# Conformer front end of a two-layer trunk: first product in high and low parts, the wide convolution wholly on the matrix engine

## The chip, the cores and the metric

The kernel runs on one NeuronCore of a Trainium2 chip. The engines are TensorE (PE in the profile; PEld is its weight load), VectorE (DVE), ScalarE (ACT) and GpSimd (POOL); SyncE (SP) issues the large transfers. Each engine works through its own instructions in order and waits for the others by semaphores. The metric is the device time of one execution in microseconds (us). Three executions of the kernel before took 2595.46, 2598.17 and 2601.18 us; the median is 2598.17 us.

## The reference

The input is one sequence of 256 positions and 2048 channels in float32. Two layers follow each other; each has a token mixer and a dense squared-ReLU MLP, each with a pre-RMSNorm whose shift, scale and gate come from a conditioning vector c. Only the first mixer, the Conformer convolution module, is touched by the change:

```
def conformer_conv(u, w_pw1, b_pw1, w_dw, b_dw, ln_g, ln_b, w_pw2, b_pw2):
    v = u @ w_pw1 + b_pw1
    a, gt = jnp.split(v, 2, axis=-1)
    v = a * jax.nn.sigmoid(gt)
    v = causal_dwconv(v, w_dw, b_dw)
    v = jax.nn.silu(layernorm(v, ln_g, ln_b))
    return v @ w_pw2 + b_pw2
...
        mod = (sc @ w_mod[i] + b_mod[i])[:, None, :]
        sh1, sc1, g1, sh2, sc2, g2 = jnp.split(mod, 6, axis=-1)
        u = rmsnorm(h, norm_mix_g[i]) * (1 + sc1) + sh1
```

So u is 256 x 2048, w_pw1 is 2048 x 4096, the depthwise convolution has 31 taps over each of 2048 channels, and w_pw2 is 2048 x 2048. The modulation vectors (sh1, sc1, g1, sh2, sc2, g2) are products of silu(c) with a 2048 x 12288 matrix per layer.

## The kernel before

Activations lie with channels on the 128 partitions and the 256 positions along the row, four channel tiles to a group. A channel tile of 128 is called a row here, as in the code; there are 16. Weights come in tiles of 128 x 2048 numbers (1 MB) through SP's queue, in program order, into three buffers `w32`.

**Modulation vectors.** `gemv` (L263 to L293) reads a 1 MB tile of w_mod into one of the buffers `wm` (2) or `hid` (4). Most tiles are multiplied with silu(c) and summed by one DVE instruction (L289). The groups in `PE_GROUPS` go through four PE products with 32 columns (L280), and after every fourth tile a copy, four transposes (L301) and a short DVE sum in `columns`. POOL adds the bias (`mod_done`, L317 to L320). A list of such tiles, `EARLY`, is worked off by `pump` at the rates `RATE_PW1`, `BETWEEN`, `RATE_PW2`, `RATE_OPEN` and so on.

**The first product** (w_pw1) has eight column blocks of 512 (two rows of a, two of the gate) and four quarters of the 2048 inputs. `native` multiplies in plain float32 (L709): 16 products of 128 x 128 by 128 x 256 for each weight tile. The opening takes blocks 0 to 3 together, quarter by quarter, since the shift and scale of a quarter (eight w_mod tiles, all summed on DVE) are loaded between the weights; `vectors` (L576) makes u of a quarter from them. Blocks 4 to 7 follow one by one.

**The gate** (`glu`) is a sigmoid on ACT (L590) and one DVE instruction (L592), which writes the row into a padded buffer `vpad`, kept behind u in the same tile.

**The wide convolution** takes two ways. Eight rows (`TE_ROWS`) go to PE: POOL's queue copies the row into four shifted copies (`shift`, L632; rows 14 and 15 by PE in `lift`, L640) and loads a matrix of taps from memory (L624), and `convolve` (L655) makes 32 products with 32 columns. The other eight rows are done by `conv`: 28 taps on ACT (L602), summed by DVE (L611), three more on DVE. `close` (L669, L672) subtracts a common mean and squares; `moments` and `direct` sum for the LayerNorm.

**The second product** (w_pw2) and the later ones split each weight tile in two halves, each into a high part (`wh`, ACT, L358) and a low part (`wl`, DVE, L360), three buffers each. With x split the same way, `products` in its `single` form makes three PE products of 128 x 256 for one: wh by x high, wh by x low, wl by x high (L373). A half of `wl` can only be written when the products of the half three places earlier have been made.

The order on each engine is made by a scheduler from program order and priorities (`high_priority`, `issue_after`); transfers keep program order.

Of the kernel before, what the change touches and what calls it, by code (L numbers as in the profile page):

```python
# [15 lines left out]
P = 128  # L16
# [13 lines left out]
def spread(n, slots):  # L30
# [16 lines left out]
RATE_PW1 = [1, 1, 1, 1, 1, 2, 1, 1, 1, 2, 1, 1, 1, 1, 0, 0]  # L47
BETWEEN = 5
# [11 lines left out]
ACT_TAPS = 28  # L60


TE_ROWS = (3, 5, 6, 7, 9, 13, 14, 15)
# [3 lines left out]

EARLY = [(0, s, 4 * g + i) for s, g in ((G1, 0), (G1, 1), (G1, 2), (SC2, 0), (SH2, 0), (SH2, 1)) for i in range(4)]
_te = [(0, SH2, 5 + i) for i in range(11)]
_ve = [(0, G1, 12 + i) for i in range(4)] + [(0, SC2, 4 + i) for i in range(12)]  # L70
EARLY = EARLY[:-3] + [v for pair in zip(_ve[:9], _te) for v in pair] + _te[9:] + _ve[9:]


PE_GROUPS = {(0, SH2, g) for g in range(4)}
# [5 lines left out]
    ("b_pw1", 32), ("w_dw", 16 * TAPS), ("b_dw", 16), ("ln_g", 16), ("ln_b", 16), ("b_pw2", 16),  # L80
# [21 lines left out]
def layout(inp):  # L102
# [8 lines left out]
    for ct in TE_ROWS[:-2]:  # L111
        order[ct] = order[ct].reshape(32, 4).T.reshape(-1)
    order = order.reshape(-1)
    par = np.concatenate([
        _cols(a["c"]), _cols(a["b_mod"]), _cols(a["norm_mix_g"]), _cols(a["norm_mlp_g"]),
        _cols(a["final_norm_g"]), _cols(a["cf_b_pw1"]),
        a["cf_w_dw"][0].reshape(TAPS, NT, P).transpose(2, 1, 0).reshape(P, -1),
# [19 lines left out]
    taps = np.zeros((32, D), f)  # L137
    taps[:TAPS] = a["cf_w_dw"][0].reshape(TAPS, D)
    quad = np.zeros((len(TE_ROWS), 4, 32, 8, 4, 32), f)
    for i, ct in enumerate(TE_ROWS):  # L140
        w = taps[:, ct * P:(ct + 1) * P].reshape(4, 8, 32, 4)
        if ct >= NT - 2:
            w = w.reshape(4, 8, 4, 32).transpose(0, 1, 3, 2)
        for p in range(32):
            quad[i, :, p, :, :, p] = w[:, :, p, :]
    return {
        "quad": quad.reshape(len(TE_ROWS), P, 8, P),
# [29 lines left out]
class Trunk:  # L177
# [44 lines left out]
    def prologue(self):  # L222
# [26 lines left out]
        self.xpad = self.const("xpad", [P, 5 * (3 + T)])  # L249
        self.sel = self.t("bT", [P, T], bufs=1)[:, :P]  # L250
# [12 lines left out]
    def gemv(self, layer, seg, ct, parts=((0, 4),)):  # L263
# [8 lines left out]
        if (layer, seg, g) in PE_GROUPS:  # L272
# [10 lines left out]
            if i == 3:  # L283
                row = self.t("t2", [P, 512], bufs=3)
                with self.tc.issue_after(self.act):
                    nc.scalar.copy(out=row, in_=self.row_sums)
                self.rows_left.append([self.row_sums, row, m, layer, seg, g, 0])
# [63 lines left out]
    def split_half(self, w, i, hi_after=None, lo_after=None):  # L351
        nc = self.nc
        s = slice(2 * i, 2 * i + 2)
        wh = self.wp.tile([P, 2, 512], F32R, tag="wh", name=self.nm("wh"), bufs=3)
        wl = self.wp.tile([P, 2, 512], F32R, tag="wl", name=self.nm("wl"), bufs=3)
# [192 lines left out]
    def conformer(self):  # L548
# [12 lines left out]
        room = [self.b("u", [P, 8 * T]) for _ in range(4)]  # L561
        u = [v[:, :4 * T].rearrange("p (k t) -> p k t", k=4) for v in room]

        W = T + TAPS
        vpad = [v[:, 4 * T + i * W:4 * T + (i + 1) * W] for v in room for i in range(3)]
        for v in vpad:
            nc.gpsimd.memset(v[:, :TAPS - 1], 0.0)
            nc.gpsimd.memset(v[:, W - 1:], 0.0)
        dd = [self.b("acc", [P, 4, T], bufs=5) for _ in range(4)]
        st = {"m0": None, "sq": {}, "sums": None}  # L570

        quad = self.b("acc", [P, 8, P], bufs=5)
        copies = self.xpad[:, :4 * LONG].rearrange("p (c t) -> p c t", c=4)
        parts, late = {}, []

        def vectors(g, t0, t1):  # L576

            for t in range(t0, t1):
# [4 lines left out]
                nc.scalar.activation(out=u[g][:, t, :], in_=m, func=AF.Identity,  # L583
                                     bias=self.mod_tile(0, SH1, g)[:, t:t + 1])

        def glu(ct, bank):

            with self.tc.high_priority(AHEAD_GLU if ct < NT - 3 else AHEAD_CHAIN):
# [101 lines left out]
        def native(blocks, done, pump=None, hook=None, rows=()):  # L690
# [24 lines left out]
            if len(blocks) == 1:  # L715
                for g in range(4):
                    if hook and g == 3:
                        hook()
# [657 lines left out]
```

## Time and profile before

| quantity | value |
|---|---|
| median of three executions | 2598.17 us |
| the profiled execution | 2596.74 us |
| its span | 2594.8 us |
| PE busy over the span | 2541.4 us (98%) |
| DVE busy | 1911.0 us (74%) |
| ACT busy | 1308.0 us (50%) |
| mean DMA rate | 256 GB/s |
| first product begins / blocks 0 to 3 end | 37.19 / 152.23 us |
| `lift` of rows 14 and 15 begins | 288.13 us |
| second product begins | 311.24 us |

Times are in us from the start of the span. A view by lines groups instructions by source line, engine and tile; "idle before" names what ended the wait. A plain float32 product appears as two records of PE. The chain of waits follows the work that ended last backwards. The view by windows gives the busy time of each engine in a stretch, the granted PE clock and the share of time the DMA engines were busy.

### The profile page before, as it was taken

The numbers are of one execution on the slowest core, as the hardware profiler recorded it, in microseconds if no ns is written. First come the engines' busy times: TensorE is split into PE (matmuls) and PEld (weight loads), VectorE is DVE, ScalarE is ACT, GpSimd is POOL, SyncE is SP. The second block draws the span as 40 slices with busy tenths as digits, with TensorE's granted clock in tenths as the row PEclk, the third lists the DMA queues.
The fourth block names the chain that finished last, engine by engine and source line by source line (L and its number), as shares of the span: only waits on it lengthen the run. The fifth ranks groups of instructions, "written<-read, shape, count | busy, mean of one in ns | idle before, by whom it ended". The sixth has DMA issues, their size and how long they took to land.

```text
span 2594.8 us, 36897 instructions
## 1 busy us (share of the span) xinstructions
PE 2541.4 (98%) x14671; PEld 2183.1 (84%) x14671; DVE 1911.0 (74%) x2460; ACT 1308.0 (50%) x2009; POOL 147.5 (6%) x212
## 2 busy tenths in 40 slices
PE   6999999999999999999999999999999999999998
PEld 5887698988888888888888888888998888888886
DVE  6579577877878878888777777888885555565565
ACT  2067453544434434447777767644454444443443
POOL 0011000000000000000000000000001101101000
PEclk8999999999999999999999999999999999999999
DMA  9988797788888878856555555678765555555554
GB/s 404 381 321 305 266 345 292 276 325 324 311 327 319 321 291 345 320 215 218 185 188 176 176 185 186 243 297 324 284 252 195 190 184 195 192 182 195 193 182 144
DMA packets 94895, 664.85 MB, mean 256 GB/s; under 512 B 10977, under 2 KB 10977, under 8 KB 16769
## 3 DMA queue, kind: packets, MB, share of 16 engines
q1 hardware_dynamic: 89138, 643.87, 67.5%
q0 software_dynamic: 5152, 16.97, 2.3%
q8 instruction: 115, 1.88, 0.3%
q10 hardware_dynamic: 432, 1.66, 0.2%
q14 instruction: 58, 0.48, 0.1%
HBM read 657.02 MB, written 2.20 MB: 254 GB/s over the span
## 4 chain that ended last, share of the span: by engine, by line
PE 95%; DVE 2%; DMA 2%; ACT 1%; issue 0%; POOL 0%; ACTq 0%; SPq 0%; DVEq 0%
PE mm L373 59%; PE mm L427 8%; PE mm L429 8%; PE mm L428 8%; PE mm L709 7%; DMA hid<-wmT 1%; PE mm L655 1%; PE ms L709 1%; PE ms L1288 1%; PE ms L280 1%; DVE wl L360 0%; DVE hid L289 0%; PE ms L1257 0%; PE ms L1267 0%; PE ms L509 0%
## 5 line engine op out<-in xcount | busy, mean ns | idle before, releaser
L373 PE MATMUL mm<-u,wh 128*128 128x512 f32 (+1 forms) x4544 | 1374.2, 365 | 6.4 <-ACT u L482 2.3
L358 ACT CAST wh<-w 128x1024 fp32r<-128x1024 f32 x768 | 806.7, 1051 | 991.5 <-PE mm L373 612.1
L360 DVE TENSOR_TENSOR wl<-w,wh 128x1024 fp32r<-128x1024 f32 x768 | 941.2, 1228 | 495.6 <-ACT wh L358 492.0
L373 PE MATMUL mm<-u,wl 128*128 128x256 f32 x3840 | 1080.0, 282 | 0.1
L373 PEld LDWEIGHTS mm<-u,wh 128*128 128x128 f32 x4544 | 812.8, 190 | 157.8 <-issue 10.2
L373 PEld LDWEIGHTS mm<-u,wl 128*128 128x128 f32 x3840 | 730.2, 190 | 5.6 <-issue 3.4
L427 PE MATMUL mm<-wh,hid 128*128 128x512 f32 x896 | 350.9, 392 | 0.0
L429 PE MATMUL mm<-wh,hid 128*128 128x512 f32 x896 | 348.9, 389 | 0.0
L428 PE MATMUL mm<-wl,hid 128*128 128x512 f32 x896 | 348.8, 389 | 0.0
L289 DVE SCALAR_TENSOR_TENSOR wm<-wm,scb 128x2048 f32<-128x2048 f32 x133 | 303.7, 2283 | 11.0 <-DMA wm<-wmT 10.7
L709 PE MATMUL mm<-u,w 128*128 128x256 f32 x864 | 192.3, 384 | 19.1 <-ACT u L583 19.1
L709 PEld LDWEIGHTS mm<-u,w 128*128 128x128 f32 x864 | 165.2, 192 | 45.3 <-ACT u L583 19.9
L427 PEld LDWEIGHTS mm<-wh,hid 128*128 128x128 f32 x896 | 168.2, 188 | 35.7 <-issue 1.0
L428 PEld LDWEIGHTS mm<-wl,hid 128*128 128x128 f32 x896 | 168.2, 188 | 35.4 <-issue 0.7
L429 PEld LDWEIGHTS mm<-wh,hid 128*128 128x128 f32 x896 | 168.2, 188 | 35.2
L373 PE MATMUL mm<-hid,wh 128*128 128x512 f32 (+1 forms) x576 | 183.7, 376 | 2.8 <-DVE acc L913 2.8
L373 PE MATMUL mm<-hid,wl 128*128 128x256 f32 x512 | 143.9, 281 | 0.0
L289 DVE SCALAR_TENSOR_TENSOR hid<-hid,scb 128x2048 f32<-128x2048 f32 x43 | 98.2, 2285 | 40.7 <-DMA hid<-wmT 40.6
L373 PEld LDWEIGHTS mm<-hid,wh 128*128 128x128 f32 x576 | 104.9, 190 | 24.0 <-DVE acc L913 3.2
L317 POOL TENSOR_TENSOR mod<-mod,par 128x4 f32<-128x4 f32 x46 | 39.5, 858 | 1139.8 <-DVE wm L289 905.7
L602 ACT ACTIVATE taps<-u,par 128x256 f32<-128x256 f32 x224 | 93.0, 501 | 9.4 <-DVE taps L611 7.0
L373 PEld LDWEIGHTS mm<-hid,wl 128*128 128x128 f32 x512 | 97.4, 190 | 0.4 <-issue 0.2
(251 smaller groups left out, 1599.7 us busy)
## 6 DMA issues: line engine op xcount, KB each, us to landing
w<-w SPq DMA_DIRECT2D x256, 1024.0 KB, 4.9
wm<-wmT SPq DMA_DIRECT2D x139, 1024.0 KB, 7.3
w<-win SPq DMA_DIRECT2D x80, 1024.0 KB, 4.9
hid<-wmT SPq DMA_DIRECT2D x53, 1024.0 KB, 11.1
w<-pw SPq DMA_DIRECT2D x46, 1024.0 KB, 7.5
w<-wout SPq DMA_DIRECT2D x32, 1024.0 KB, 6.7
acc<-ac_d POOLq DMA_DIRECT2D x16, 512.0 KB, 7.5
xpad<-u POOLq DMA_DIRECT2D x24, 131.5 KB, 9.0
```

The source lines that it names most:

```text
L280: self.pe = nc.tensor.matmul(self.row_sums[32 * t:32 * t + 32, :], lhsT=self.scol[:, kt:kt + 1].broadcast_to([P, 32]), rhs=w[:, t * 512:(t ...
L289: self.sum = nc.vector.scalar_tensor_tensor(out=w, in0=w, scalar=1.0, in1=self.scb, op0=ALU.mult, op1=ALU.mult, accum_out=m[:, i:i + 1]).ins
L317: nc.gpsimd.tensor_tensor(out=m, in0=m, in1=b, op=ALU.add)
L358: nc.scalar.copy(out=wh, in_=w[:, s, :])
L360: nc.vector.tensor_tensor(out=wl, in0=w[:, s, :], in1=wh.bitcast(F32), op=ALU.subtract)
L373: self.pe = self.nc.tensor.matmul(out, lhsT=lhsT, rhs=rhs, skip_group_check=True, **kw).ins
L427: mm(banks[q], lhsT=hi, rhs=wh[:, k, :], start=g == 0 and t == 0, stop=False)
L428: mm(banks[q], lhsT=hi, rhs=wl[:, k, :], start=False, stop=False)
L429: mm(banks[q], lhsT=lo, rhs=wh[:, k, :], start=False, stop=g == 3 and t == 3)
L602: st["tap"] = nc.scalar.activation(out=p4[:, q, :], in_=vp[:, k + q:k + q + T], func=AF.Identity, scale=self.col("w_dw", ct * TAPS + k + q ...
L655: self.pe = nc.tensor.matmul(o[32 * c:32 * c + 32, :], lhsT=w[:, k, 32 * c:32 * c + 32], rhs=r[:, c, k:k + T], start=k == 0, stop=k == 7, ...
L709: self.pe = nc.tensor.matmul(o, lhsT=w[:, t, j * P:(j + 1) * P], rhs=u[g][:, t, :], start=g == 0 and t == 0 and j < 2, stop=g == 3 and t == 3,
```

## The change

The first product takes the split form of the later ones: u is written in high and low parts (`split_x`, ACT and DVE), each weight tile of w_pw1 is split in two halves, and each product becomes three. All 16 rows of the convolution go through `convolve`; `conv` on ACT and DVE is gone. The matrix of taps is no longer read from memory: one DVE instruction (`weigh`) multiplies a diagonal pattern with the taps. Rows lie unpadded in the place where the closed row will stand; `shift` copies only what exists, and zeros are written once into the two buffers of copies (one of which, with one matrix of taps, takes the two `wm` buffers during blocks 4 to 7). From the third of these weight tiles on, one row is convolved after each tile. The PE groups of the modulation change: the first two of sh1 and the last two of sh2 in place of all four of sh2. `EARLY` is reordered: 24 tiles, all for DVE, are worked off in blocks 4 to 7 (16 before), 4 in `BETWEEN` (5 before), and in the second product the next 18 hold 3 for PE (9 before).

```diff
-RATE_PW1 = [1, 1, 1, 1, 1, 2, 1, 1, 1, 2, 1, 1, 1, 1, 0, 0]
-BETWEEN = 5
+RATE_PW1 = [1, 2] * 8
+BETWEEN = 4
...
-PE_GROUPS = {(0, SH2, g) for g in range(4)}
+PE_GROUPS = {(0, SH1, 0), (0, SH1, 1), (0, SH2, 2), (0, SH2, 3)}
...
+        self.diag32 = self.xpad[:, 4 * LONG:4 * LONG + 32]
+        nc.vector.reduce_sum(out=self.diag32, in_=self.ident.rearrange("p (a j) -> p j a", a=4),
+                             axis=mybir.AxisListType.X)
...
-                nc.scalar.activation(out=u[g][:, t, :], in_=m, func=AF.Identity,
-                                     bias=self.mod_tile(0, SH1, g)[:, t:t + 1])
+                self.split_x(u[g], t, m, self.mod_tile(0, SH1, g)[:, t:t + 1])
...
-        def conv(ct):
...
+        def weigh(ct):
+            nc.vector.tensor_tensor(
+                out=quads[ct % 2].rearrange("p k (c j) -> p (k c) j", j=32),
+                in0=self.diag32.rearrange("p (o j) -> p o j", o=1).broadcast_to([P, 32, 32]),
+                in1=self.col("w_dw", ct * 32, 32).rearrange("p (k o) -> p k o", o=1).broadcast_to([P, 32, 32]),
+                op=ALU.mult)
         def shift(ct):
-            weigh(ct, quad, nc.gpsimd)
             for i in range(4):
-                nc.gpsimd.dma_start(out=copies[32 * i:32 * i + 32], in_=vpad[ct % 12][:, 8 * i:8 * i + LONG])
+                k = TAPS - 1 - 8 * i
+                n = min(T, LONG - k)
+                nc.gpsimd.dma_start(out=copies[ct % 2][32 * i:32 * i + 32, :, k:k + n],
+                                    in_=dd[ct // 4][:, ct % 4, :n])
...
+        def products(banks, b, g, parts, ts):
+            for j in (0, 2, 1, 3):
+                o = banks[j % 2][:, (j // 2) * T:(j // 2 + 1) * T]
+                for t in ts:
+                    self.products(o, parts[t // 2], u[g], t % 2, t, slice(j * P, (j + 1) * P), True,
+                                  g == 0 and t == 0 and j < 2, g == 3 and t == 3)
+                if g == 3 and ts[-1] == 3 and j >= 2:
+                    glu(2 * b + j - 2, banks[j - 2])
...
+        for b in range(FIRST, 8):
+            if b >= 6:
+                moments(b - 6)
+            own = [self.bank(self.mm, "mm") for _ in range(2)]
+            for g in range(4):
+                w = self.load_w(a["pw1"][b, g])
+                self.pump(pump(g))
+                pair = [ahead(w, k) for k in range(2)]
+                for k in range(2):
+                    products(own, b, g, pair, (2 * k, 2 * k + 1))
+                if b == FIRST and g < 2:
+                    continue
+                ct = next(row)
+                if ct == 1:
+                    common()
+                    close(0)
+                convolve(ct)
+                weigh(ct + 2)
+                if ct + 2 < LIFTED:
+                    shift(ct + 2)
+                if ct:
+                    close(ct)
```

Line numbers of the changed kernel are a few lower: its L286 is L289 before (sum of a w_mod tile), L357 is L360 (low part of a weight half), L566 is L580 (`nrm`, the scaled row), L483 writes the low part of u, L578 is L592 (gate), L594 is L632 (copies). Two places show what moves.

The order on DVE around the third quarter of the opening. `hid` and `wm` are w_mod tiles, `nrm` the scaled rows, `wl` low parts; the first fence is before, the second the change.

```order
L289 SCALAR_TENSOR_TENSOR hid_404,mod_380<-hid_404,scb 128x2048
L289 SCALAR_TENSOR_TENSOR hid_407,mod_384<-hid_407,scb 128x2048
L289 SCALAR_TENSOR_TENSOR wm_428,mod_380<-wm_428,scb 128x2048
L289 SCALAR_TENSOR_TENSOR hid_431,mod_384<-hid_431,scb 128x2048
L289 SCALAR_TENSOR_TENSOR hid_452,mod_380<-hid_452,scb 128x2048
L580 SCALAR_TENSOR_TENSOR nrm_462<-h_77,mod_380,t_16_160 128x256
```

```order
L286 SCALAR_TENSOR_TENSOR wm_728,mod_600<-wm_728,scb 128x2048
L286 SCALAR_TENSOR_TENSOR hid_731,mod_604<-hid_731,scb 128x2048
L357 TENSOR_TENSOR wl_737<-w_98_734,wh_736 128x1024
L357 TENSOR_TENSOR wl_741<-w_98_734,wh_740 128x1024
L286 SCALAR_TENSOR_TENSOR hid_792,mod_600<-hid_792,scb 128x2048
L566 SCALAR_TENSOR_TENSOR nrm_802<-h_77,mod_600,t_16_161 128x256
L566 SCALAR_TENSOR_TENSOR nrm_806<-h_77,mod_600,t_16_161 128x256
L286 SCALAR_TENSOR_TENSOR wm_798,mod_604<-wm_798,scb 128x2048
L483 SCALAR_TENSOR_TENSOR u_165<-nrm_802,mod_604,u_165 128x256
```

Before, DVE met only w_mod tiles and scaled rows there; now two low parts stand between each pair of w_mod tiles, and each row of u ends with a DVE instruction.

The order on DVE of the change where blocks 0 to 3 end and block 4 begins. The `mm` and `ms` tiles are the sums of blocks 0 to 3 in PSUM (two for a block), `hid_1386` is a w_mod tile, and `w_178` is the first weight tile of block 4. Before, the plain product of block 4 needed no DVE instruction of its own.

```order
L578 SCALAR_TENSOR_TENSOR acc_1237<-mm_237,par,a_1320 128x256
L286 SCALAR_TENSOR_TENSOR hid_1386,mod_1388<-hid_1386,scb 128x2048
L578 SCALAR_TENSOR_TENSOR acc_1238<-mm_238,par,a_1329 128x256
L578 SCALAR_TENSOR_TENSOR acc_1238<-mm_239,par,a_1338 128x256
L578 SCALAR_TENSOR_TENSOR acc_1238<-ms_464,par,a_1347 128x256
L578 SCALAR_TENSOR_TENSOR acc_1238<-ms_465,par,a_1356 128x256
L357 TENSOR_TENSOR wl_1391<-w_178_1384,wh_1390 128x1024
```

The gates of all eight rows, the last of which need the end of block 3's products, now stand ahead of the low part that block 4's first products read.

On ACT of the change, in the same place: `a_1347` and `a_1356` are the sigmoids of the last two rows, and `wh` high parts of the first two weight tiles of block 4.

```order
L575 ACTIVATE a_1347<-ms_464,par 128x256
L355 CAST wh_1394<-w_178_1384 128x1024
L355 CAST wh_1454<-w_184_1446 128x1024
L575 ACTIVATE a_1356<-ms_465,par 128x256
L355 CAST wh_1458<-w_184_1446 128x1024
```

Two casts now stand between the last two sigmoids.

More of the change, by code (lines that the diff above doesn't have):

```diff
@@ L560, in conformer @@
         nc.scalar.activation(out=r, in_=ps, func=AF.Sqrt, scale=1.0 / D, bias=self.eps)
[L561 to L569, printed above, removed]
+        u = [self.b("u", [P, 4, 2 * T], F32R) for _ in range(4)]
         st = {"m0": None, "sq": {}, "sums": None}
-        quad = self.b("acc", [P, 8, P], bufs=5)
-        copies = self.xpad[:, :4 * LONG].rearrange("p (c t) -> p c t", c=4)
-        parts, late = {}, []
+        parts = {}
         def vectors(g, t0, t1):
@@ new lines, in ahead, with vec @@
+        def ahead(w, i, room=None):
+            with self.tc.high_priority(self.ahead):
+                return self.split_half(w, i, room=room)
+        def vec(g, t):
+            for s in (SC1, SH1):
+                self.gemv(0, s, 4 * g + t, ((0, 2), (2, 3), (3, 4)) if g == 3 else ((0, 4),))
+        for t in range(4):
+            vec(0, t)
+            if t == 1:
+                with self.tc.issue_after(self.sum):
+                    nc.vector.reciprocal(r, r)
+        self.columns()
@@ new lines, in conformer @@
+        vectors(3, 0, 2)
+        room = lambda tag: self.b("acc", [P, 2, 512], F32R, bufs=5)
+        last = []
+        for i in range(FIRST):
+            if i == 2:
+                vec(3, 2)
+                vectors(3, 2, 3)
+            w = self.load_w(a["pw1"][i, 3])
+            first = ahead(w, 0, room)
+            last.append([first, ahead(w, 1, None if i < 3 else room)])
+            products(banks[i], i, 3, last[i], (0, 1))
+        vec(3, 3)
+        vectors(3, 3, 4)
+        dd = [self.b("acc", [P, 4, T], bufs=5) for _ in range(2)]
@@ new lines, in conformer @@
+        for t in (2, 3):
+            for i in range(FIRST):
+                products(banks[i], i, 3, last[i], (t,))
+        dd += [self.b("acc", [P, 4, T], bufs=5) for _ in range(2)]
+        spot = [self.b("wm", [P, D], bufs=2) for _ in range(2)]
+        quads = [self.b("acc", [P, 8, P], bufs=5), spot[1][:, :8 * P].rearrange("p (k c) -> p k c", k=8)]
+        copies = [v[:, :4 * LONG].rearrange("p (c t) -> p c t", c=4) for v in (self.xpad, spot[0])]
+        W = T + TAPS
+        padded = {ct: spot[0][:, 4 * LONG + i * W:4 * LONG + (i + 1) * W] for i, ct in enumerate((14, 15))}
@@ L768, in conformer @@
+        for v in copies:
+            nc.gpsimd.memset(v[:, :, :TAPS - 1], 0.0)
+            nc.gpsimd.memset(v[:, :, LONG - 1:], 0.0)
+        for v in padded.values():
+            nc.gpsimd.memset(v[:, :TAPS - 1], 0.0)
+            nc.gpsimd.memset(v[:, W - 1:], 0.0)
+        self.rings = ("hid",)
         self.jobs += EARLY
@@ L848, in conformer @@
         with self.tc.high_priority(AHEAD_CHAIN):
-            half = self.split_half(there[0], 0, tap, d15)
+            half = self.split_half(there[0], 0, st["gate"], d15)
         with self.tc.issue_after(self.pe):
```

214 lines of the change are left out of this document (63 added, 151 removed).

## The prediction

> **What bounds the kernel now.** I read the view by windows first, cut at the borders of the Conformer's stages, then PE's timeline and the chain of waits inside them. The columns of the windows are: stretch, length, busy time of PE, PEld, DVE, ACT and POOL, granted PE clock, DMA share, GB/s.
>
> ```profile
> 0.00:97.00 97.00, 74.39 (x297) 60.39 (x298) 60.61 (x61) 17.28 (x37) 6.33 (x52) 0.91 0.99 409
> 97.00:152.20 55.20, 55.20 (x256) 48.59 (x257) 27.26 (x39) 9.36 (x20) 1.86 (x4) 1.00 0.80 318
> 152.20:288.10 135.90, 135.90 (x931) 109.58 (x930) 116.03 (x141) 103.27 (x256) 21.17 (x35) 1.00 0.90 308
> 288.10:311.20 23.10, 20.86 (x267) 10.73 (x266) 9.68 (x17) 8.15 (x17) 0.48 (x5) 1.00 0.53 206
> 311.20:416.30 105.10, 105.06 (x836) 95.19 (x837) 78.59 (x97) 53.26 (x82) 4.43 (x8) 0.98 0.93 356
> ```
>
> Up to 97 us the transfers set the pace (share 0.99). From 97 to 288 us and from 311 to 416 us PE has no gap; there a microsecond on PE is a microsecond of time, and work of DVE and ACT costs nothing as long as it stays in time. After 416 us the change alters no instruction of the layers, only how many w_mod tiles are left (seven fewer, all on a DVE that is not the bound there); I cost that at nothing, and if it should count, it is a gain.
>
> **The change part by part.** The rows for PE, first from its timeline, then from the chain (start, length, what):
>
> ```profile
> 96.87 20.99 PE L709 MATMUL mm<-u,w 128*128 128x256 f32 x96 [1.75 <-ACT u L583]
> 152.23 7.07 PE L709 MATMUL mm<-u,hid 128*128 128x256 f32 x32
> ```
>
> ```profile
> 166.21 3.61 PE mm L655 x64
> ...
> 311.24 5.81 PE mm L373 x32
> ...
> 327.50 5.75 PE mm L373 x48
> 333.26 0.99 PE ms L280 x8
> 334.25 11.71 PE mm L373 x96
> ...
> 365.60 0.44 PE ms L301 x4
> ```
>
> *One weight tile.* Plain: 32 records, 7.0 us (20.99 / 3). Split: 48 products, 5.855 us (11.71 / 2). So splitting saves PE 1.15 us a tile, 18 us in the opening's 16 tiles and 18 us in the 16 of blocks 4 to 7. One row of the convolution costs 3.6 us of PE.
>
> *Blocks 4 to 7.* After: 16 x 5.855 = 93.7, 14 rows x 3.6 = 50.4, the sums for the LayerNorm and the common mean 2.3 as now: 146.4 us, against 135.9 (which holds 6 rows). That is +10.5: eight more rows on PE (+28.8) cost more than the split returns (-18.3). Nothing covers it, since PE had no gap here. The work of ACT and DVE that goes away was hidden. It stays +10.5 only if DVE and the copies keep up. DVE, from its timeline (start, length; the distance of starts is what counts):
>
> ```profile
> 435.45 2.28 DVE L289 SCALAR_TENSOR_TENSOR hid<-hid,scb 128x2048 f32<-128x2048 f32 x1
> 437.66 0.08 DVE L289 DVE_READ_ACCUMULATOR hid<-hid,scb 128x1 f32 x1
> 437.66 1.22 DVE L360 TENSOR_TENSOR wl<-w,wh 128x1024 fp32r<-128x1024 f32 x1
> 438.80 0.48 DVE L486 SCALAR_TENSOR_TENSOR u<-nrm,mod,u 128x256 fp32r<-128x256 f32 x1
> ```
>
> A w_mod tile takes DVE 2.21 us, a low part 1.14, a row of 256 some 0.4. In blocks 4 to 7: 24 x 2.21 = 53, 32 x 1.14 = 36.5, 14 matrices of taps at about a low part's size 17, 30 small rows 12: 118 of 146 us, 81% (now 116 of 136). Between two convolutions PE needs 9.45 us, DVE 7.4 on average; the low parts stand one to one and a half tiles ahead. In time. Transfers: 40 tiles of 1 MB at 2.5 us (below) are 100 of 146 us.
>
> The copies, in the view of tile `xpad` over this stretch:
>
> ```profile
> L632 POOL DMA_DIRECT2D xpad<-u x24: 550/550/612, 150.3 to 266.7; - x24
> DMA to landing us min/median/max: 7.7/9.0/11.4
> ```
>
> Four issues of 0.55 us after the convolution that frees the buffer, then at worst 11.4 us: 13.5 us. In the change the buffer is used again after two weight tiles and one row, 15.3 us. Covered, by 2 us at worst; the matrix of taps no longer sits ahead of them in POOL's queue. Unpadded rows only shorten these copies: nothing.
>
> *The opening.* Its transfers are the same 48 tiles plus input. Their pace, from DVE waits that a landing ended:
>
> ```profile
> 19.31 2.29 DVE L289 SCALAR_TENSOR_TENSOR wm<-wm,scb 128x2048 f32<-128x2048 f32 x1 [0.19 <-DMA wm<-wmT]
> ...
> 44.25 2.29 DVE L289 SCALAR_TENSOR_TENSOR hid<-hid,scb 128x2048 f32<-128x2048 f32 x1 [1.77 <-DMA hid<-wmT]
> 46.74 2.29 DVE L289 SCALAR_TENSOR_TENSOR wm<-wm,scb 128x2048 f32<-128x2048 f32 x1 [0.19 <-DMA wm<-wmT]
> ```
>
> The third tile lands at 19.1, then one each 2.5 us. The last w_mod tile of the third quarter is the 32nd in SP's order, so 91.6 us; sum, bias, high and low part of u put PE's start on that quarter at 96 us at the earliest. It is 96.87 now. From there PE has two quarters left: 8 x 5.855 = 46.8 us, which ends the opening at 143.7, against 152.2. That is the best case, -8.5. But DVE now carries 32 low parts and 16 low rows here (36.5 + 6.4) and only gives eight w_mod tiles to PE (-17.7). By the order printed above, from 69 us (where the last low part of the first quarter has waited for its buffer) DVE has eight w_mod tiles (17.7), eight low parts (9.1) and about 2 us of rows and a wait for POOL's bias before u begins: 98, the first two rows of u complete at 102. Following rows and the ring of three halves to the end, I get the last row of u at 146 and PE's end at 152.7. Each small wait was put on its bad side, so I take 150.5, between the two but nearer to the walk: -1.7, bounds -8.5 and +1. The PE groups' 8 us of products are in PE's gaps here.
>
> *Entry into block 4, a new wait.* As printed, the sigmoid of the last row stands behind two casts on ACT, its gate ahead of block 4's first low part on DVE, and PE's third product reads that low part. Rows for cast, sigmoid and gate (line, tile, count | busy, mean ns | idle before):
>
> ```profile
> L358 ACT CAST wh<-w 128x1024 fp32r<-128x1024 f32 x80 | 83.7, 1048 | 103.2 <-PE mm L373 82.1 <-PE mm L429 16.0 <-issue 2.5
> L592 DVE SCALAR_TENSOR_TENSOR u<-mm,par,a 128x256 f32<-128x256 f32 x14 | 6.7, 481 | 13.3 <-ACT a L590 13.3
> L590 ACT ACTIVATE a<-mm,par 128x256 f32<-128x256 f32 x14 | 6.5, 466 | 10.2 <-PE mm L709 10.2
> ```
>
> The sigmoid of row 6 can start 0.7 us before the end of block 3 (six products of 0.122). Then 0.47 + 2 x 1.0 + 0.47 on ACT, 0.48 for the gate, 1.22 for the low part: 4.0 us after the end, of which 0.24 is covered by two products. I take +4; bounds 2.4 (no casts between) and 6 (with the slow clock below). Now there is none: the record at 152.23 follows without idle.
>
> *Lift and LayerNorm, 288 to 311 us.* Same instructions on PE and the same chain; one matrix of taps (1.2 us of DVE) ahead of the copies fits into the 3.7 us of `lift`. The tiles of `BETWEEN` lie in its gap, four or five alike: nothing, +-1.
>
> *Second product.* Six w_mod tiles fewer on PE (3 for 9) at 0.99 and two turned groups fewer at 0.44: -6.8, PE being the bound. DVE takes over: 32 low parts 36.5, LayerNorm rows 11.3 (six wide at 1.14, twelve at about 0.4), 15 tiles 33.2, evacuation 11 (28 at 0.4): 92 of 99 us. My walk finds two late low parts of 0.3 us: -6.3, bounds -6.8 and 0.
>
> Sum on the span: -1.7 + 4 + 10.5 + 0 - 6.3 = +6.5, 2594.8 to 2601.3. The profiled execution adds 1.9 around it (2596.74) and lies 1.4 under the median, so the forecast for the median is 2598.17 + 6.5 = **2604.7 us**, slower by 0.25%.
>
> **Rivals.** *The opening gains in full (not slower).* If DVE works ahead so that u of the third quarter comes at 96 us, the opening ends at 143.7, and with the entry at its low bound: -8.5 + 2.4 + 10.5 - 6.8 = -2.4, 2595.8. For it: the transfers allow it, and after 58 us, when the weights of the first quarter have landed, DVE has 28 low parts (31.9), 16 w_mod tiles (35.4) and some 12 us of rows left, 79 us, which could end at 137. Against: DVE's strict order, with the ring of three halves in it. It decides from u at about 99 us. If the entry cost nothing either, 2593.4; below lies only a gain that I don't see.
>
> *DVE becomes the bound in the second product.* At 92 of 99 us every late w_mod tile (2.5 us of transfer) delays the low part behind it. Against: DMA needs 34 tiles, 85 of 99 us. If the gain of 6.3 is lost: +12.8, 2611.
>
> *The slow clock after gaps.* The row at 311.24 shows 32 products in 5.81 us where 3.9 is the pace: 1.9 lost after thin products and 2.28 us of waiting, while 1.75 us before 96.87 cost nothing. The entry (3.8 us idle) and the start of the third quarter (some 6) are such gaps: 1.9 to 3.8, so 2606.6 to 2608.5. [...]
>
> *The copies come late.* If landing took 4 us more than the worst row, each of 14 rows would wait 2 us: +28, 2633. Against: DMA is no fuller than now.
>
> **How the numbers follow.** About 0.2% (5.2 us) is what a measurement of this kernel can tell from no change; the borders are 2593.0 and 2603.4. Forecast 0.47, opening in full 0.28, slow clock 0.12, DVE in the second product 0.09, copies 0.04. The forecast itself spans 2599 to 2609, two fifths of it under 2603.4 (0.19). The rival on the opening gives 0.13 to faster, since its sums have small errors of their own and it lies near that border, and 0.15 to the same. The others are slower. Faster 0.13, same 0.34, slower 0.53. Range for 8 in 10: 2593 to 2612; the likeliest case's own is 2599 to 2609.
>
> **What would show it.** Blocks 4 to 7 take 146 us between the first product of block 4 and `lift`, with PE closed except at the entry; if convolutions wait for copies, POOL or DVE will be named as releaser. The first product of block 4 should be followed by a gap of some 4 us ended by a low part. The opening's end near 150 us, with PE waiting for u of the third quarter near 100 us, shows DVE as its pace; an end near 144 shows the rival. The second product should take 98 to 100 us for 105. I am wrong if the opening gains more than 6 us, or if the split products run slower than 5.9 us a tile when row convolutions stand between them.

## The result and the profile after

The changed kernel takes 2618.38 us (median of six executions, 2613.8 to 2623.66) against 2597.26 us of the kernel before on the same chip (six, 2595.17 to 2601.18). The ratio is 1.0082, interval 1.0066 to 1.0097: slower by 21 us. The prediction had 2604.7 us and a range up to 2612, so the direction was right and the size, 6.5 us, was not. The profiled execution took 2623.66 us (span 2621.9), the slowest of the six; the stages below sum to its own 27.1 us, some 6 us more than the medians differ by, so that much is peculiar to this execution.

The stages are cut at four instructions of PE: the first product of block 4, the first of `lift`, the first of the second product and the first of the layer's MLP.

| stage, us | before | after | difference | predicted |
|---|---|---|---|---|
| opening, to block 4 | 152.23 | 158.30 | +6.1 | -1.7 |
| block 4 to `lift`, with the entry wait | 135.90 | 168.33 | +32.4 | +14.5 |
| `lift` to second product | 23.11 | 23.09 | 0 | 0 |
| second product to the MLP | 114.75 | 103.67 | -11.1 | -6.3 |
| the rest | 2168.8 | 2168.5 | -0.3 | 0 |

PE's timeline of the changed kernel has the marks and the waits (start, length, what, idle before and who ended it):

```profile
101.11 0.74 PE L370 MATMUL mm<-u,wh 128*128 128x256 f32 x4 [3.44 <-ACT wh L355]
...
103.90 0.58 PE L370 MATMUL mm<-u,wh 128*128 128x256 f32 x1 [0.61 <-DVE u L483]
...
119.18 0.74 PE L370 MATMUL mm<-u,wh 128*128 128x256 f32 x4 [1.98 <-ACT wh L355]
...
158.30 0.64 PE L370 MATMUL mm<-u,wh 128*128 128x256 f32 x4
162.21 0.39 PE L370 MATMUL mm<-u,wl 128*128 128x256 f32 x1 [3.28 <-DVE wl L357]
...
326.63 3.74 PE L604 MATMUL mm<-wm,ident 128*32 128x263 f32 x64
...
453.39 1.10 PE L370 MATMUL mm<-u,wh 128*128 128x256 f32 x3 [1.24 <-ACT u L482]
```

Before, PE had not one gap from 96.87 to 288 us. Now it waits at the third quarter of the opening, at the entry into block 4, and in blocks 4 to 7. The windows of the changed kernel (columns as in the prediction):

```profile
97.00:158.30 61.30, 53.77 (x391) 52.26 (x390) 50.94 (x64) 24.52 (x34) 3.68 (x13) 0.89 0.84 338
158.30:326.60 168.30, 154.53 (x1700) 127.29 (x1702) 115.53 (x119) 49.59 (x74) 39.23 (x63) 0.96 0.94 290
326.60:349.70 23.10, 19.98 (x263) 10.92 (x254) 10.67 (x19) 6.73 (x15) 0.48 (x5) 1.00 0.27 101
349.70:446.90 97.20, 96.11 (x792) 92.84 (x793) 91.01 (x109) 50.39 (x77) 7.85 (x8) 1.00 0.94 371
```

Two things stand out. In blocks 4 to 7 the DMA engines are busy 0.94 of the time and yet move only 290 GB/s; in the second product, at the same share, they move 371. And the granted clock is below 1 in the opening (0.89) and in blocks 4 to 7 (0.96), where it was 1.00 before.

Who waits in blocks 4 to 7, by the view of waits of PE and of DVE (us in total, times, longest):

```profile
PE mm L370 <- DVE wl L357: 13.8, 6, 4.3
...
DVE hid L286 <- DMA hid<-wmT: 29.7, 9, 8.4
DVE wl L357 <- ACT wh L355: 11.5, 7, 2.4
```

PE names DVE, but DVE is itself held by w_mod tiles that have not landed: a low part is queued behind one in DVE's strict order. The chain of waits says the same: in this stretch four landings of w_mod tiles hold 62.7 of its 169 us (19.5, 16.8, 11.7 and 14.6 us), more than any other single group, though PE's own work together holds more. Two of the four:

```profile
207.24 1.24 DVE wl L357
208.47 0.02 issue
208.49 0.33 SPq L341
208.82 0.05 issue
208.87 19.48 DMA hid<-wmT
...
230.67 1.15 DVE wl L357
231.82 0.02 issue
231.84 0.33 SPq L341
232.16 0.05 issue
232.21 16.81 DMA hid<-wmT
```

A low part frees a weight buffer, SP issues the next transfers, and the w_mod tile among them needs 12 to 19 us. The queues of this stage, after (158.3 to 326.6 us) and then before (152.2 to 288.1 us); columns are packets, MB, share of the 16 engines' time; q1 carries the 1 MB tiles of SP, q0 what POOL issues (after, the copies alone; before, 21 copies and five matrices of taps of 512 KB from memory); `x24` and `x16` are transfers with their median us to landing:

```profile
q1 hardware_dynamic: 5707, 41.55, 76.3%
q0 software_dynamic: 2683, 7.00, 17.0%
...
hid<-wmT SPq DMA_DIRECT2D x24, 1024.0 KB, 16.2
w<-pw SPq DMA_DIRECT2D x16, 1024.0 KB, 10.5
```

```profile
q1 hardware_dynamic: 5069, 35.89, 71.6%
q0 software_dynamic: 1872, 5.86, 17.5%
...
w<-pw SPq DMA_DIRECT2D x14, 1024.0 KB, 5.7
hid<-wmT SPq DMA_DIRECT2D x11, 1024.0 KB, 11.0
```

After, a packet of q0 holds 2.6 KB in the mean (two expectations below say about 1 KB). Worked out: the copies take 17.0% of 168.3 = 28.6 us for 7.00 MB, 245 GB/s. The tiles take 128.4 us for 41.55 MB, 324 GB/s; before it was 97.3 us for 35.89 MB, 369 GB/s. In the opening, without copies, they had run at 409 to 420.

### The profile page after: what moved, and what is told of

Same layout as the page of the kernel before. It is cut to its first block, busy times and chain, and to the rows that moved or that the text cites. A ratio compares the mean times of both kernels' runs of the same rounds, so it can differ in the third digit from the quotient of the medians.

```text
span 2621.9 us, 38896 instructions
## 1 busy us (share of the span) xinstructions
PE 2552.7 (97%) x15695; PEld 2204.0 (84%) x15695; DVE 1936.1 (74%) x2469; ACT 1281.9 (49%) x1850; POOL 162.9 (6%) x222
## 4 chain that ended last, share of the span: by engine, by line
PE 90%; DVE 4%; DMA 4%; issue 1%; ACT 1%; POOL 0%; SPq 0%; ACTq 0%; DVEq 0%
PE mm L370 61%; PE mm L424 8%; PE mm L426 8%; PE mm L425 8%; DMA hid<-wmT 3%; DVE wl L357 1%; PE mm L620 1%; DVE hid L286 1%; PE ms L1265 1%; DMA w<-pw 0%; ACT wh L355 0%; DVE wm L286 0%; PE ms L555 0%; DMA acc<-ac_d 0%; PE ms L370 0%
## 5 line engine op out<-in xcount | busy, mean ns | idle before, releaser
L370 PE MATMUL mm<-u,wh 128*128 128x512 f32 (+1 forms) x5392 | 1540.0, 354 | 16.4 <-ACT wh L355 7.2
L357 DVE TENSOR_TENSOR wl<-w,wh 128x1024 fp32r<-128x1024 f32 x827 | 1012.1, 1228 | 522.4 <-ACT wh L355 519.0
L355 ACT CAST wh<-w 128x1024 fp32r<-128x1024 f32 x827 | 867.1, 1050 | 1039.2 <-PE mm L370 620.1
L370 PE MATMUL mm<-u,wl 128*128 128x256 f32 x4264 | 1203.4, 284 | 17.0 <-DVE wl L357 16.9
L370 PEld LDWEIGHTS mm<-u,wh 128*128 128x128 f32 x5392 | 953.7, 193 | 172.0 <-issue 13.9
L370 PEld LDWEIGHTS mm<-u,wl 128*128 128x128 f32 x4264 | 815.9, 192 | 23.9 <-DVE wl L357 20.5
L286 DVE SCALAR_TENSOR_TENSOR wm<-wm,scb 128x2048 f32<-128x2048 f32 x121 | 276.3, 2284 | 4.9 <-DMA wm<-wmT 4.9
L286 DVE SCALAR_TENSOR_TENSOR hid<-hid,scb 128x2048 f32<-128x2048 f32 x55 | 125.5, 2285 | 39.1 <-DMA hid<-wmT 32.9
L1021 POOL TENSOR_TENSOR wm<-wm,t 128x512 f32<-128x512 f32 x24 | 43.2, 1824 | 498.0 <-DVE t L1019 382.3
L1083 DVE SCALAR_TENSOR_TENSOR a<-xpad,par,a 128x256 f32<-128x256 f32 x144 | 63.8, 479 | 1.1 <-ACT a L1080 0.3
L482 ACT ACTIVATE u<-nrm,mod 128x256 fp32r<-128x256 f32 x64 | 29.9, 502 | 50.6 <-DVE mod L310 24.1
## 6 DMA issues: line engine op xcount, KB each, us to landing
hid<-wmT SPq DMA_DIRECT2D x68, 1024.0 KB, 11.7
```

The lines of the kernel that those rows point to most:

```text
L286: self.sum = nc.vector.scalar_tensor_tensor(out=w, in0=w, scalar=1.0, in1=self.scb, op0=ALU.mult, op1=ALU.mult, accum_out=m[:, i:i + 1]).ins
L355: nc.scalar.copy(out=wh, in_=w[:, s, :])
L357: nc.vector.tensor_tensor(out=wl, in0=w[:, s, :], in1=wh.bitcast(F32), op=ALU.subtract)
L370: self.pe = self.nc.tensor.matmul(out, lhsT=lhsT, rhs=rhs, skip_group_check=True, **kw).ins
L482: self.hi = nc.scalar.activation(out=hi, in_=src, func=AF.Identity, bias=bias).ins
L1021: nc.gpsimd.tensor_tensor(out=h, in0=h, in1=v, op=ALU.add)
```

## The experiments

The theory after the result: in blocks 4 to 7 the DMA engines are full, by 40 tiles and 56 copies together, and late w_mod tiles hold up low parts in DVE's order. Rivals: the ring of four buffers for w_mod tiles, or DVE's own work in its strict order. For the opening: DVE's low parts delay u, against transfers or the slow clock alone. For the second product: the order of the w_mod tiles, against the split first product.

A table of the borders of all profiled kernels, us from the span's start. A run given with one time is one execution; what is read from it is its stages, not a difference of a few us in its time.

| kernel | block 4 begins | `lift` | second product | MLP | span |
|---|---|---|---|---|---|
| before | 152.2 | 288.1 | 311.2 | 426.0 | 2594.8 |
| after | 158.3 | 326.6 | 349.7 | 453.4 | 2621.9 |
| no_copies | 155.3 | 308.1 | 331.2 | 434.8 | 2603.9 |
| short_sums | 155.9 | 315.7 | 338.7 | 443.6 | 2611.3 |
| tiles16 | 155.7 | 310.1 | 333.1 | 436.3 | 2607.0 |
| native_open | 157.4 | 334.3 | 357.4 | 461.2 | 2623.3 |
| open_no_low | 147.4 | 316.1 | 339.1 | 442.6 | 2607.1 |
| entry16 | 154.1 | 310.0 | 333.0 | 437.5 | 2606.3 |
| copies_halved | 156.0 | 342.5 | 365.6 | 468.8 | 2639.1 |
| copies_act | 156.1 | 328.0 | 351.1 | 454.5 | 2624.6 |
| before_groups | 152.4 | 288.3 | 311.4 | 419.0 | 2590.2 |
| before_groups2 | 158.6 | 294.5 | 317.6 | 422.2 | 2590.9 |

**no_copies.** The changed kernel without the copies; the buffers hold zeros.

```diff
         def shift(ct):
-            for i in range(4):
-                k = TAPS - 1 - 8 * i
-                n = min(T, LONG - k)
-                nc.gpsimd.dma_start(out=copies[ct % 2][32 * i:32 * i + 32, :, k:k + n],
-                                    in_=dd[ct // 4][:, ct % 4, :n])
+            return
...
```

> The changed kernel without the 56 transfers that copy rows 0 to 13 into the shifted buffers (the buffers are zeroed once and stay zero, so the convolution of these rows is left out in value, not in its PE instructions). Theory 'DMA is full': in blocks 4 to 7 the copies (7 MB in packets of about 1 KB, 17% of the DMA engines' time) and the 40 tiles together fill the DMA engines; without the copies these blocks fall from 164 us to 146 to 150, the landing of a w_mod tile from 16 us to under 12, and the whole from 2622 to about 2605. Rival 'ring of four': w_mod tiles have only the four hid buffers there and stand ahead of the weights in SP's queue, so the wait is for buffers and not for bandwidth; then these blocks stay at 160 or more. Rival 'DVE's order': DVE's strict order holds PE; then they also stay.

One execution: 2605.76 us. From block 4 to `lift` 152.8 us instead of 168.3; after the entry wait 148.9, against my 146.4. The queues and landings in that stage:

```profile
q1 hardware_dynamic: 5851, 42.54, 71.4%
...
hid<-wmT SPq DMA_DIRECT2D x24, 1024.0 KB, 8.2
```

The same tiles now take 109.1 us of the engines (390 GB/s) instead of 128.4, and w_mod tiles land in 8.2 us. So the copies cost twice: 28.6 us of their own, and 19 us by which the tiles slow down beside them. DVE's order and the ring are as in the changed kernel, and PE's only wait left is the one at the entry. So neither rival holds the stage by itself; DVE's order is the way by which a late transfer reaches PE.

**short_sums.** The changed kernel with the sum of a w_mod tile taken over 128 of its 2048 columns in this stage (the rest of each sum is left out): DVE is relieved, the transfers stay.

```diff
-        self.sum = nc.vector.scalar_tensor_tensor(out=w, in0=w, scalar=1.0, in1=self.scb, op0=ALU.mult,
+        n = self.short
+        self.sum = nc.vector.scalar_tensor_tensor(out=w[:, :n], in0=w[:, :n], scalar=1.0, in1=self.scb[:, :n], op0=ALU.mult,
...
```

> The changed kernel with each w_mod sum of blocks 4 to 7 on DVE taken over 128 of its 2048 columns (the rest of these sums is left out); every transfer stays. It takes some 2 us of DVE from each of 24 tiles, 48 us in all, and frees each buffer 2 us earlier. Theory 'DMA is full': blocks 4 to 7 stay at 158 to 164 us, for the bytes are the same. Rival 'DVE's order': they fall to about 146. Rival 'ring of four': they fall by a part, to about 152, since buffers come back earlier.

2613.12 us; block 4 to `lift` 159.8 us. From 162 to 320 us the two queues hold the engines for 97% of the time (81.5% and 15.5%) and a w_mod tile lands in 20.2 us; PE now waits for copies (two waits, 5.5 us) and for low parts only 2.6 us. Though DVE is busy for only 69 us of it, the stage is still 24 us longer than before and 13 us above PE's own sum of 146.4, so the limit is the transfers. It is 8.5 us shorter than in the changed kernel, 3.4 of this at the entry, so DVE's work is not without a share. The wait at the entry is gone here, because the schedule came out otherwise: the first low part of block 4 starts at 154.76, ahead of the last gates (155.90).

**tiles16.** Sixteen w_mod tiles in the stage instead of 24; `EARLY` is reordered for it.

```diff
-RATE_PW1 = [1, 2] * 8
+RATE_PW1 = [1] * 16
...
```

> The changed kernel with 16 w_mod tiles instead of 24 in blocks 4 to 7 (one for each weight tile), the four PE tiles of sh2 next in the gap of the LayerNorm, and the eight others later. Theory 'DMA is full': 8 MB less at 2.5 to 3 us each brings blocks 4 to 7 from 164 to 146 to 150 us; the second product loses nothing, since it holds about as many DVE tiles as now; the whole comes to about 2603, ratio to before near 1.003. Rival 'ring of four': the same sign, but the landing of a w_mod tile stays near 16 us. Rival 'DVE's order': about 150, with low parts still named as releaser.

2610.3 us (2607.83 to 2617.24), ratio to the kernel before 1.0053, interval 1.0035 to 1.0071. Block 4 to `lift` is 154.3 us with the entry wait, 150.4 without, a little above the 146 to 150 expected, and w_mod tiles land in 10.1 us: the stage does what the theory says. The time does not: 2603 was expected. Between the profiled executions it falls by 14.9 us, between the medians by 8.1, since the 164 us that I started from came from the slowest execution of the changed kernel. What this edit does not reach stays: the opening is 3.5 us longer than before, and the entry costs 3.4.

**copies_act.** The copies issued by ACT, on another queue.

```diff
-                nc.gpsimd.dma_start(out=copies[ct % 2][32 * i:32 * i + 32, :, k:k + n],
+                nc.scalar.dma_start(out=copies[ct % 2][32 * i:32 * i + 32, :, k:k + n],
```

> The changed kernel with the 56 copies issued by ACT instead of POOL: same bytes and pieces, another queue. If the price of the copies (245 GB/s while they have the engines, 7 MB in 29 us) belongs to POOL's queue, it falls: blocks 4 to 7 at 150 to 156 us, and the time 8 to 14 us lower. If it belongs to the short pieces whatever the queue, the share of the engines' time stays near 17% and the stage at 160 to 168 us. If ACT is held up by the issues (each waits for a gate or for a convolution that frees the buffer, with casts of weight halves queued behind it), PE is seen waiting for high parts of weights and the stage is longer than 168 us.

2626.34 us; block 4 to `lift` 171.9 us. The queues:

```profile
q1 hardware_dynamic: 5843, 42.49, 73.5%
q10 hardware_dynamic: 8064, 7.02, 17.4%
```

The queue changes and the price does not: 17.4% of 171.9 is 29.9 us for 7.02 MB, as much as through POOL (28.6), though in three times as many packets (8064 for 2683). The stage is longer than the 160 to 168 us expected of an unchanged price, but not for the reason that I had named: PE does not wait for high parts, it waits 8.8 us before convolutions and 6.8 us for low parts.

**copies_halved.** Each copy as two transfers of half the columns.

```diff
+                h = n // 2
+                for x, y in ((0, h), (h, n)):
-                nc.gpsimd.dma_start(out=copies[ct % 2][32 * i:32 * i + 32, :, k:k + n],
-                                    in_=dd[ct // 4][:, ct % 4, :n])
+                    nc.gpsimd.dma_start(out=copies[ct % 2][32 * i:32 * i + 32, :, k + x:k + y],
+                                        in_=dd[ct // 4][:, ct % 4, x:y])
```

> The changed kernel with each copy of a row sent as two transfers of half the columns: 112 transfers instead of 56, the same bytes, pieces of about 0.5 KB instead of 1 KB. It asks what a copy costs the DMA engines. If they are paid by the piece, the copies' share of the engines' time (16.7% of a stretch of 172 us, 29 us) goes to about 50 us, and since the engines are full (share 0.92 to 0.99), blocks 4 to 7 grow from 164 us to 180 to 190 us. If they are paid by the byte, the share stays at 15 to 18% and the stage at 160 to 168 us; POOL issues 4.4 us instead of 2.2 us for a row, which no wait on PE should show.

2640.88 us; block 4 to `lift` 186.4 us, the length that the price by the piece would give, but for another reason. The queue of the copies over this stage, and POOL's wait (158 to 345 us):

```profile
q0 software_dynamic: 3584, 7.02, 12.3%
```

```profile
POOL xpad L596 <- DMA xpad<-acc: 48.6, 14, 6.7
```

12.3% of 186.4 is 22.9 us for the same 7.02 MB: smaller pieces cost no more. The packets grew in number only from 2683 to 3584, so this run tests the price by the piece less sharply than copies_act does. What got longer is the way: POOL now waited for transfers that had just been issued (48.6 us in this group alone, 41.0 in its twin), and PE waited 25 us before convolutions. So the price here is not by the piece; that it is simply by the byte is not shown beyond that, since the engines were less crowded (share 0.79). But at 245 GB/s in the changed kernel, against 390 for the tiles in no_copies, the copies are not as cheap by the byte as large tiles.

**open_no_low.** No low parts of weights in blocks 0 to 3; the third product reads the high part (the low part's share is left out).

```diff
-        wh, wl = room("wh"), room("wl")
+        wh = room("wh")
+        wl = room("wl") if low else wh
...
```

> The changed kernel, but in blocks 0 to 3 no low part of the weights is made and the third of the three products reads the high part in its place: same instructions on PE, same transfers, 32 fewer DVE instructions of 1.1 us in the opening. Left out: the share of the weights' low part in blocks 0 to 3. It asks what sets the end of the opening at 157.1 us. If DVE's low parts do (they stand in one strict order with the w_mod tiles and with u of the third and fourth quarter, and hold the buffers of weight halves), u of the third quarter comes at 96 to 98 us and the opening ends at 144 to 148. If the transfers or the gaps' slow clock alone do, u still comes at about 102 to 104 us and the end stays at 154 to 158. Blocks 4 to 7 after it as in the changed kernel, 160 to 166 us, because copies and transfers are not touched there.

2608.9 us. The opening ends at 147.4 us instead of 158.3 (155.3 to 156.1 in the five other runs that leave the opening alone): DVE's low parts, with the buffers that they hold, were its pace, as the prediction had it. With them half of PE's waits went (3.4 us for 7.4 from 90 us on) and most of the slow clock (0.97 from 97 us on, for 0.89), so the two are not told apart here. Blocks 4 to 7 keep their length (164.8 us after the wait), as they should.

**native_open.** The changed kernel with plain products in blocks 0 to 3 (u and the weights there are not split for the product), the rest as changed.

```diff
+                    if b < FIRST:
+                        self.pe = nc.tensor.matmul(o, lhsT=parts[:, t, j * P:(j + 1) * P],
+                                                   rhs=u[g][:, t, :T].bitcast(F32),
...
```

> The changed kernel with the plain float32 product in blocks 0 to 3 (on the high part of u alone, so the low part's share of these blocks is left out), and the split product from block 4 on. Theory 'DVE and the slow clock set the opening': without 32 low parts on DVE (36 us) and without PE's gaps, the opening ends at 150 to 152 us instead of 157, though PE has 18 us more to do there; the wait at the entry of block 4 stays at 4 to 5 us. Rival 'the transfers set it': it stays at 157 or gets later.

2625.16 us, a miss: block 4 begins at 157.4, not 150 to 152. PE's third quarter starts at 100.19 us, where it starts at 96.87 in the kernel before: the second four of the eight w_mod tiles that the change puts on PE stand among the first quarter's products, from 45 to 57 us, where PE was full before (15.0 of 15 us). From 100.19 on PE waits only 1.5 us. Blocks 4 to 7 take 176.9 us here, longer than in the changed kernel, with 46.9 MB of tiles in place of 41.6 and a share of 0.98: tiles that the opening had not fetched fell into the full stage, as the theory would have it.

**entry16.** tiles16, and block 4's first weight tile split ahead of the last gates.

```diff
...
-            with self.tc.high_priority(self.ahead):
+            with self.tc.high_priority(self.ahead + more):
...
-                pair = [ahead(w, k) for k in range(2)]
+                pair = [ahead(w, k, more=2000 if b == FIRST and g == 0 else 0) for k in range(2)]
```

> The kernel with 16 w_mod tiles instead of 24 in blocks 4 to 7, and in addition the two halves of block 4's first weight tile are split at a higher priority, so that their casts and low parts stand ahead of the last sigmoids and gates of block 3 on ACT and DVE. If the wait of 3.3 us at block 4's third product comes from that order alone, it is gone or under 1 us, block 4 runs on without a gap, and the time is 4 us less than with 16 tiles alone: about 2606. If the weight tile itself lands late, or the wait only moves to the gates' readers, the gap stays near 3 us and the time near 2610.

2608.06 us. The entry wait is gone, so its cause was the order on ACT and DVE, as in short_sums. But `lift` begins where it did (310.0 against 310.1 us): PE waits 5.7 us for a low part that is ready at 262.6 us, and the clock is 0.83 from 260 to 280 us. Of the 3.3 us regained, and 1.6 more in the opening, nothing is left at that border.

**before_groups.** The kernel before, with the first group of sh1 instead of the first of sh2 on PE and `EARLY` reordered to fit; its first product and convolution are untouched.

```diff
...
-PE_GROUPS = {(0, SH2, g) for g in range(4)}
+PE_GROUPS = {(0, SH1, 0), (0, SH2, 1), (0, SH2, 2), (0, SH2, 3)}
...
```

> The kernel before with the plain first product and its convolution untouched, only the groups of w_mod tiles that go through PE changed: the first group of sh1 (in the opening, where PE has gaps) in place of the first group of sh2, so four PE tiles fewer in the second product. If the gain of the second product (105.1 to 97.2 us) is due to the w_mod tiles on PE that it lost and has nothing to do with the split first product, each tile gives about 1 us: the second product is 4 to 5 us shorter, the opening the same to 1 us longer, time 2592 to 2594. If DVE, which gets these tiles, is near its bound there, the second product stays at 104 to 105 and the time at 2597.

2592.94 us (twelve executions, 2590.33 to 2597.97), ratio 0.9981, interval 0.9971 to 0.999: **faster than both kernels**, by 5.0 us or 0.2% than before. From the second product's start to the MLP it takes 107.6 us for 114.75, and the opening 0.1 us more, since in its first 97 us PE has gaps (busy 74.4 us of them in the kernel before). That is 7.1 us where 4 to 5 were expected, and about 1.9 of it is the clock: 2.27 us of idle ahead of the second product were followed by a clock of 1.00, where the kernel before had 0.57 after 2.28 us (below). In this profile 2.4 us are lost again after the start of the MLP.

**before_groups2.** The kernel before with the changed kernel's groups and about its order of w_mod tiles.

```diff
...
-PE_GROUPS = {(0, SH2, g) for g in range(4)}
+PE_GROUPS = {(0, SH1, 0), (0, SH1, 1), (0, SH2, 2), (0, SH2, 3)}
...
```

> The kernel before with its plain first product, its convolution and its copies, but with the changed kernel's groups (first two of sh1, last two of sh2 on PE) and about its order of w_mod tiles (16 in blocks 4 to 7, 5 between, 3 on PE and 24 on DVE in the second product). If the change's two gains, the second product (-7.9) and the start of the MLP (-3.3), belong to the order of the w_mod tiles alone, they appear here: second product 97 to 99 us, time -6 to -10 after 0 to +4 for eight PE tiles in an opening that PE fills from 97 us on: 2588 to 2592, faster than both kernels. If the gains hang on the split first product, the second product stays near 105 and the time at 2597 or above.

2594.95 us (eleven, 2590.82 to 2597.51), ratio 0.9985, interval 0.9977 to 0.9994. Second product and MLP start together are 10.2 us shorter (104.5 for 114.75), nearly the changed kernel's 11.1. So that gain belongs to the groups and the order of the w_mod tiles and needs no split first product. But the opening ends 6.4 us later, above the 0 to +4 expected, and the time misses the 2588 to 2592: the second group's tiles come between 45 and 60 us, where PE had been full in the kernel before; there they take 4.2 us and PE is idle 3.6 us.

## Why the prediction was right or wrong

**Blocks 4 to 7: the step that failed.** The prediction counted "40 tiles of 1 MB at 2.5 us (below) are 100 of 146 us" and held the copies covered by their landing times. The number of tiles was right; their pace was wrong for this stage, and the engines' time for the copies was put at nothing. The 2.5 us come from the opening, where no copies run. The view of queues of the kernel before, quoted above, would have warned of it: 41.55 MB at its 369 GB/s are 112.6 us, 7.0 MB of copies at the 246 GB/s of its second queue (17.5% of 135.9 us for 5.86 MB, nearly half of it matrices of taps) are 28.5; that is 141 of 146 us, 96%. It would not have given the 168 us that came. Landings grew long in the full stage (w_mod from 11.0 to 16.2 us, and 8.2 without the copies), and DVE's strict order turns a late w_mod tile into a late low part: here the step "In time" failed with it. The row of the window before already said 0.90 at 308 GB/s, and I read only the 0.90. Measured without copies the stage after the entry is 148.9 us, so the sum of PE's work (146.4) was nearly right. With them it is 164.4: the term was short by 18 us, which alone is more than the whole miss of the median (13.7). PE's idle time is 10.5 us of this after the entry; 5.0 us is PE at a lower clock (0.96 against 0.99 in no_copies, busy 154.5 us against 149.5), and 2.5 us is the sum of PE's work itself.

**"Against: DMA is no fuller than now"**, in the rival of late copies, fails with it. That its price (28 us) is near what came is chance, for it is 2 us of waiting for each of 14 rows, and in the changed kernel PE waits for no copy in blocks 4 to 7. The tiles are late, not the copies. The experiments show that the copies come next once something else gives way (5.5 us of waits in short_sums).

**The opening.** The walk along DVE's order gave two rows of u at 102 us (PE began on the second at 103.9, in tiles16 at 103.1) and an end of 152.7, and the forecast took 150.5; the rival with the full gain fell, since DVE did set the pace (open_no_low). The end came 5 to 8 us later (158.3 in this profile, 155.3 to 156.1 in five runs with the same opening, so some 2.5 us belong to this execution), and the slow clock is of the size to account for it. Three kernels, from 97 us to the start of block 4:

```profile
97.00:155.71 58.71, 51.84 (x384) 50.44 (x385) 50.09 (x63) 24.54 (x34) 3.67 (x13) 0.91 0.84 339
```

```profile
97.00:154.14 57.14, 50.55 (x385) 48.95 (x385) 48.97 (x61) 24.73 (x32) 2.86 (x11) 0.94 0.88 352
```

The first is tiles16, the second entry16, whose edit moves two splits at the end of the opening; the third is the changed kernel's row above. Lost clock is (1 - 0.89) x 61.3 = 6.7 us after, 5.3 in tiles16, 3.4 in entry16. Taken from the ends, it leaves 151.6, 150.4 and 150.7. PE's busy time says the same: 53.8, 51.8 and 50.6 us for work of 46.8 (8 x 5.855). So the loss of the rival "the slow clock after gaps" (0.12) came in addition to the forecast, a term that its sum put at nothing. I had priced it at 1.9 us a gap from one row; the two gaps of the opening together cost 3.4 to 6.7. Of the two places that the rival named, the start of the third quarter paid in this profile and the entry did not (last section). This correspondence is arithmetic over profiles; no run took the gaps alone away.

**Entry into block 4.** Right: a wait of 3.28 us for the low part, 3.4 us in all, forecast 4 (2.4 to 6), and entry16 confirms the order as its cause. That it does not always pay to remove it, where a full stage follows, was not foreseen.

**Lift and LayerNorm** stayed at 23.1 us, as predicted.

**Second product.** The sign and the cause were right, the size was low: -11.1 us up to the MLP, forecast -6.3. Of the difference 1.9 us is luck: before, 2.28 us of idle ahead of the second product were followed by a clock of 0.57 and 32 products in 5.81 us, where 3.9 is the pace; after, 3.14 us of idle were followed by a clock of 1.00, while in tiles16 the same 3.14 us were followed by 0.56 (products at 0.21 us instead of 0.12). The rows of w_mod products on PE over that stretch, before and after (count | busy, mean ns):

```profile
L280 PE MATMUL ms<-hid,scol 128*32 128x512 f32 x48 | 7.4, 604 | 0.0
L280 PE MATMUL ms<-wm,scol 128*32 128x512 f32 x32 | 5.3, 604 | 0.0
L301 PE MATMUL ms<-ident,t 128*128 128x128 f32 x12 | 1.9, 277 | 0.0
```

```profile
L277 PE MATMUL ms<-hid,scol 128*32 128x512 f32 x16 | 2.1, 604 | 0.0
L277 PE MATMUL ms<-wm,scol 128*32 128x512 f32 x8 | 1.1, 604 | 0.0
L298 PE MATMUL ms<-ident,t 128*128 128x128 f32 x4 | 0.6, 272 | 0.0
```

At eight records a tile these are ten tiles and now three: seven fewer, where I had counted six. The tenth stood among the sums before the MLP, a chain that I cost at nothing: it took 7.6 us from the last product (418.40) to the first of the MLP, and takes 5.7 now. Seven tiles at 0.99, two groups at 0.44 and the 1.9 us of clock are 9.7 of the 11.1 us; the rest is not resolved. DVE did not become the bound: PE waits 1.1 us for a low part there.

**The sum.** 6.1 + 32.4 - 11.1 - 0.3 is the profiled 27.1 us. Against the forecast of +6.5: opening +7.8, blocks 4 to 7 with the entry +17.9, second product -4.8, rest -0.3. The trace's own test in the prediction worked: blocks 4 to 7 had to show 146 us "with PE closed except at the entry", and did not; and split products did run slower than 5.9 us a tile: PE was busy 154.5 us in this stage for a sum of 146.4.

## What to carry to other kernels

Before a stage is filled with more transfers, add up all queues of that stage at the pace that they have there, not at the pace of a stage with one kind of transfer; here a share of 0.90 at 308 GB/s meant that the engines were nearly full with costly traffic, and 16% more bytes (48.6 MB for 41.8) in a stage planned 8% longer were too many. When a product is split, each of its halves gets a place in the order of two more engines, and a late transfer ahead of it in that order can become a wait of PE (here PE waited 10.5 us for low parts after the entry). Part of a change may be worth keeping alone: four w_mod tiles moved to where PE had gaps, with the order of the others fitted to it, gave 5 us without the rest.

## What the runs showed of the hardware

Copies within the chip's memory were dear beside large tiles: 7.0 MB took 28.6 us of all 16 engines and slowed 41.6 MB of tiles from 390 to 324 GB/s (one execution without copies beside the profiled one with them). Issued by ACT, in three times as many packets, they took 29.9 us, and the tiles ran at 336 GB/s. I had not expected the second part.

After PE's wait of 3.44 us at 101 us the products ran at 0.21 us instead of 0.12 until 109.6, and after only 1.98 us at 119.18 they did so again until 126.7. The window of these stretches in the changed kernel:

```profile
104.00:110.00 6.00, 6.00 (x30) 6.00 (x31) 6.00 (x8) 2.49 (x3) 0.00 (x0) 0.53 0.87 362
110.00:115.00 5.00, 5.00 (x44) 5.00 (x43) 4.89 (x8) 0.00 (x0) 0.43 (x6) 1.00 0.49 157
...
119.00:125.00 6.00, 5.30 (x25) 5.09 (x26) 3.89 (x4) 2.52 (x5) 0.00 (x0) 0.57 0.39 127
```

The granted clock is 0.53 in the first of the slow stretches and 0.57 in the second. So 1.98 us of waiting, with 0.52 us more at 120.44, went with as slow a clock as 3.44 us (0.52 and 0.61 more at 102.37 and 103.90), while after 1.75 us before 96.87 in the kernel before the clock is 1.00 (96.8 to 104 us).

The length of the wait alone does not decide it. The same wait at the entry into block 4, with the same instructions around it, first in the changed kernel and then in tiles16:

```profile
162.21 0.39 PE L370 MATMUL mm<-u,wl 128*128 128x256 f32 x1 [3.28 <-DVE wl L357]
162.44 0.40 PE L370 MATMUL mm<-u,wh 128*128 128x256 f32 x2
162.67 0.28 PE L370 MATMUL mm<-u,wl 128*128 128x256 f32 x1
```

```profile
159.63 0.58 PE L370 MATMUL mm<-u,wl 128*128 128x256 f32 x1 [3.28 <-DVE wl L357]
160.01 0.63 PE L370 MATMUL mm<-u,wh 128*128 128x256 f32 x2
160.44 0.41 PE L370 MATMUL mm<-u,wl 128*128 128x256 f32 x1
```

Two products take 0.23 us in the first and 0.43 us in the second: after 3.28 us of waiting the products run at 0.12 us in one execution (clock 1.00) and at 0.21 us in the other (0.57). So a price for a gap, read from one execution, is a price that another may not pay.
